# The low part of the keys in two score products: a contraction over 64 rows becomes one over 128

## The chip, the cores and the metric

The kernel runs on one core of a Trainium2 chip. The metric is the device time of one execution in microseconds (us). Lower is better. Engine names below are those of the profile: PE is TensorE's matmul, PEld its weight load, DVE is VectorE, ACT is ScalarE, POOL is GpSimd, SP is SyncE, which here only issues transfers.

## The reference

Two transformer blocks run one after the other on a sequence of 512 tokens of width 1024, all in float32. Two pieces of them matter here, the scores of the banded attention in the first block and those of the differential attention in the second:

```python
# first block: 8 query heads of width 64 on 2 key heads, a band of 128 tokens, a sink per head
s = jnp.einsum('bnqhgd,bnshd->bnhgqs', qb, kk) * (d ** -0.5)
s = jnp.where(mask[None, :, None, None], s, -jnp.inf)
p = jax.nn.softmax(jnp.concatenate([s, sink], axis=-1), axis=-1)[..., :-1]
...
# second block: 8 heads, each with two score maps (m) of width 64
s = jnp.einsum("bhmqd,bhmkd->bhmqk", qblk, kt) * scale
s = jnp.where(dist >= 0, s + bias[None, :, None], -jnp.inf)
p = jax.nn.softmax(s, axis=-1)
a = p[:, :, 0] - lam * p[:, :, 1]
return jnp.einsum("bhqk,bhkd->bhqd", a, vt)
```

Around them stand a forgetting attention in the first block, a causal convolution, a cross attention on 256 memory tokens and three gated projections in the second.

## The kernel before

All operands of the matmuls are split into a high and a low part of the type float32r, and a product is the sum of three: high by high, high by low, low by high. A score has a contraction of only 64, so its first matmul does two of the three at once. `q_stack` (L253 to L261) builds, for each half m of a 128-row tile, a tile whose 64 rows `a` hold the query's high part and whose other 64 rows `b` hold its low part. Beside it stands a key tile (`kb1`, `k1`) that holds the keys' high part in both halves. One matmul over 128 rows then gives high by high plus low by high. The third product, the query's high part by the keys' low part (`kbl`, `kl`), is a matmul of its own over the 64 rows `a` alone.

The banded attention (`swa_sc`, L640 to L667) goes over 2 key heads by 4 query blocks. A step has four pairs of such matmuls, L656 and L657, over 256 keys (128 in the first block). The differential attention (`diff_sc`, L1004 to L1023) goes over 8 heads by 4 query blocks n. A step has two pairs, L1012 and L1013, for m = 0 and m = 1, over (n + 1) * 128 keys. The forgetting attention (`fox_sc`, L736 and L737) has a pair of the same kind, only that its second matmul contracts over 68 rows. Each score lands in one of two PSUM banks (`sc_tile`), and VectorE empties it with one pass that adds the mask and takes the minimum (L658, L1015).

The instructions of each engine stand in a fixed order that a scheduler writes when the program is built. Code runs in `staged` steps (score, transposes one step later, the product with the values a step after that), and after each step `fill` advances generators that hold the large projections (`mm_T` L190, `mm_N` L199). So TensorE gets projection work between the pieces of an attention. VectorE's place in this order is shared by the softmax, the split of every weight into two parts (L171), and the convolution: 31 passes for each of 8 channel tiles (L893, L895), which the scheduler gives the lowest priority and spreads over the differential and the cross attention.

`diff_pro` (L982 to L1001) prepares a head: L992 makes the keys' low part `kl`, one VectorE pass over 128 rows. `xkv` (L1075 to L1087) loads the cross attention's keys and values of a head; the keys used the buffers of `kl` and the values a buffer of their own. `halves(m)` gives the rows `a` and `b`.

Of the kernel before, what the change touches and what calls it, by code (L numbers as in the profile page):

```python
# [11 lines left out]
F32 = mybir.dt.float32  # L12
# [3 lines left out]
ALU = mybir.AluOpType  # L16
# [43 lines left out]
class Fill:  # L60
# [6 lines left out]
    def first(self, name):  # L67
        i = [n for n, _ in self.q].index(name)
        if i > 1:
            x = self.q[i]  # L70
            del self.q[i]
            self.q.insert(1, x)
# [21 lines left out]
def two_block_kernel(ctx: ExitStack, tc: tile.TileContext, A: dict, out: bass.AP):  # L94
# [35 lines left out]
    def f(ap):  # L130
        return ap.bitcast(F32)
# [26 lines left out]

    # ---- weights: loaded in halves of the contraction, split into two float32r parts
    def load_w(src, w=CW, rp=None):  # L160
# [108 lines left out]
    def staged(items, first, second, last, lag, k):  # L269
        """first(item) at step i, second(item) at step i + lag, last(item) one step later."""  # L270
        n = len(items)
        for i in range(n + lag + 1):
            if i < n:
                first(items[i])
            if i - lag - 1 >= 0:
                last(items[i - lag - 1])
            if 0 <= i - lag < n:
                second(items[i - lag])
            fill(k(i) if callable(k) else k)
# [42 lines left out]

    # ---- norms, modulation, memory keys and values
    with ExitStack() as st:
# [95 lines left out]

        # rotary angles
        with low(-ROTP):
# [14 lines left out]

        # small per-kernel scalars
        first = dve.tensor_scalar(out=nsink, in0=V("sinks"), scalar1=-1.0, scalar2=None, op0=ALU.mult)
# [12 lines left out]

        # keys of the memory: normalised per head, transposed
        with low(LOWMK):
# [18 lines left out]

    # ---- first block
    stR = ExitStack()
# [59 lines left out]
    with ExitStack() as stS:  # L535
# [39 lines left out]

        # log of the sigmoid of the forget gate, summed along the tokens
        fs = fz.rearrange("p t h -> p (t h)")
# [62 lines left out]
        def swa_sc(it):  # L640
# [12 lines left out]
            for i in range(4):  # L653
                ps = sc_tile()
                r = slice(64 * (i % 2), 64 * (i % 2) + 64)
                pe.matmul(out=ps[:, :w], lhsT=qs[i][:, n * P:(n + 1) * P], rhs=kb1[g][:, j0 * P:j0 * P + w], start=True, stop=False)  # L656
                pe.matmul(out=ps[:, :w], lhsT=qs[i][r, n * P:(n + 1) * P], rhs=kbl[g][r, j0 * P:j0 * P + w], start=False, stop=True)  # L657
                dve.tensor_tensor_reduce(out=pt[:, i, :w], in0=ps[:, :w], in1=C("swam")[:, 256 - w:], scale=1.0,  # L658
                                         scalar=nsink[:, 4 * g + i:4 * g + i + 1], op0=ALU.add, op1=ALU.min, accum_out=mn[:, i:i + 1])
                act.activation(out=pt[:, i, :w], in_=pt[:, i, :w], func=AF.Exp, scale=-1.0, bias=mn[:, i:i + 1], accum_out=sm[:, i:i + 1])  # L660
# [129 lines left out]

    # the attention output in two float32r parts, on bytes that the attention no longer needs
    oh, ol = [None] * KT, [None] * KT
# [11 lines left out]

    # ---- output of the first block, two token tiles at a time
    with ExitStack() as st:
# [61 lines left out]

    # ---- second block: the three branches
    stV = ExitStack()  # L870
    cvp = open_pool(stV, "cvp", 2, side="right")
    with ExitStack() as st:
        wk = open_pool(st, "wk2", 2, reuse_waits="tile")
        dp = open_pool(st, "dp", 2, reuse_waits="tile")
        cm_[0] = open_pool(st, "cm2", 1, reuse_waits="tile")
        D = {}

        def glu_gen(m):
# [103 lines left out]
        def diff_pro(h):  # L982
# [5 lines left out]
            ps = transposed(kn, c0)  # L988
            kl = dp.tile([P, S], F32R, tag="kl", name="kl")
            ks = wk.tile([P, S], F32R, tag="ks", name="ks", bufs=1)  # L990
            act.activation(out=ks, in_=ps, func=AF.Copy, scale=gqk)
            dve.scalar_tensor_tensor(out=kl, in0=ps, scalar=gqk, in1=f(ks), op0=ALU.mult, op1=ALU.subtract)  # L992
            k1 = []
# [10 lines left out]
        def diff_sc(it):  # L1004
# [4 lines left out]
            for m in range(2):  # L1009
                a = halves(m)[0]  # L1010
                ps = sc_tile()
                pe.matmul(out=ps[:, :w], lhsT=q1[m][:, n * P:w], rhs=k1[m][:, :w], start=True, stop=False)  # L1012
                pe.matmul(out=ps[:, :w], lhsT=q1[m][a, n * P:w], rhs=kl[a, :w], start=False, stop=True)  # L1013
                p_ = wk.tile([P, S], F32, tag=f"dp{m}", name="dp", bufs=3 - m)
                dve.tensor_tensor_reduce(out=p_[:, :w], in0=ps[:, :w], in1=wb[:, S - w:], scale=1.0, scalar=FMAX,  # L1015
                                         op0=ALU.add, op1=ALU.min, accum_out=st_[:, 0, n, m:m + 1])
                act.activation(out=p_[:, :w], in_=p_[:, :w], func=AF.Exp, scale=-1.0, bias=st_[:, 0, n, m:m + 1], accum_out=st_[:, 1, n, m:m + 1])  # L1017
                pms.append(p_)
# [56 lines left out]
        def xkv(hd):  # L1075
            kr = dp.tile([P, 2, 256], F32, tag="kl", name="xkr")
            vr = dp.tile([P, 2, 256], F32, tag="xvr", name="xvr", bufs=1)
            nc.scalar.dma_start(out=kr, in_=kT_d[:, 2 * hd:2 * hd + 2, :])
# [132 lines left out]

    # ---- gates, projections, the weighted sum of the branches
    with ExitStack() as st:
# [219 lines left out]
```

## Time and profile before

| what | us |
|---|---|
| median of 3 runs | 1214.6 (1213.52 to 1215.86) |
| span of the profiled execution, first to last instruction | 1212.1 |
| TensorE busy | 1180.0 (97% of the span) |
| VectorE busy | 924.2 (76%) |
| ScalarE busy | 554.4 (46%) |
| GpSimd busy | 208.1 (17%) |

The profiled execution's own time is its span; the runs come out some 2.5 us above it, which is what lies before the first and after the last instruction, and what one execution differs from another. The banded attention lies at 131 to 204 us of the span, the forgetting attention at 217 to 313, the output of the first block up to 381, the differential attention's scores at 417 to 721, the cross attention up to 877, and after that come the projections of the three branches. TensorE's granted clock is at the higher of its two levels (2.4 GHz) from the banded attention to the end. A matmul's duration in the profile is longer than what it costs: matmuls follow each other before the one ahead has ended, so what a matmul costs is read from its start to the start of the next.

### The profile page before, as it was taken

The page shows a single profiled execution, that of the slowest core. Times are in us where ns is not written, and L with a number is a line of the kernel's source. Part 1 is how long each engine was busy: PE and PEld are TensorE (multiplying, and loading weights), DVE is VectorE, ACT ScalarE, POOL GpSimd, SP SyncE. Part 2 cuts the span into 40 slices and gives each one's busy share as a digit, 9 for nine tenths or more (in the row PEclk, how much of TensorE's full clock was granted, in tenths as well). Part 3 has the DMA queues.
Part 4 walks back from the last instruction along what each step waited for, and adds up shares of the span by engine and source line. Part 5 has one row for each costly group of instructions (what it writes and reads, how often), then busy time and mean ns, then how long its engine had stood idle before and what let it go on. Part 6 is the DMA issues. An engine that isn't in the chain of part 4 may idle for free.

```text
span 1212.1 us, 18966 instructions
## 1 busy us (share of the span) xinstructions
PE 1180.0 (97%) x6960; PEld 1018.9 (84%) x6960; DVE 924.2 (76%) x2047; ACT 554.4 (46%) x1173; POOL 208.1 (17%) x157
## 2 busy tenths in 40 slices
PE   7979999999999999999999999999999999999998
PEld 6868887878899988988888887988888888888898
DVE  6997766898776698998989989999793586553241
ACT  7556566557664354444545443543432245132230
POOL 1434200000021212020021221122010131111020
PEclk9989999999999999999999999999999999999999
DMA  8765312453474423323233333333446765432242
GB/s 334 263 214 153 98 49 74 150 158 109 128 238 150 125 70 97 104 88 113 88 112 90 111 107 122 112 106 122 148 134 215 268 207 190 124 104 89 88 125 83
DMA packets 61965, 165.43 MB, mean 136 GB/s; under 512 B 7120, under 2 KB 15568, under 8 KB 60848
## 3 DMA queue, kind: packets, MB, share of 16 engines
q1 hardware_dynamic: 36560, 122.41, 31.9%
q10 hardware_dynamic: 25312, 41.82, 10.0%
q8 instruction: 55, 0.90, 0.3%
q14 instruction: 38, 0.31, 0.1%
HBM read 136.80 MB, written 20.58 MB: 130 GB/s over the span
## 4 chain that ended last, share of the span: by engine, by line
PE 82%; DVE 7%; DMA 1%; issue 1%; ACT 1%; POOL 0%; ACTq 0%; POOLq 0%; DVEq 0%; SPq 0%
PE mm L190 46%; PE mm L199 22%; PE sc L1013 2%; PE tp L752 2%; DVE cv L895 1%; PE pv L1046 1%; PE sc L1012 1%; PE pv L695 1%; DVE wl L171 1%; PE tp L266 1%; PE pv L774 1%; PE sc L657 1%; PE pv L1191 1%; PE tp L240 1%; PE tp L225 1%
## 5 line engine op out<-in xcount | busy, mean ns | idle before, releaser
L169 ACT CAST wh<-raw 128x512 fp32r<-128x512 f32 x372 | 215.1, 620 | 226.5 <-PE mm L190 87.4
L171 POOL TENSOR_TENSOR wl<-raw,wh 128x512 fp32r<-128x512 f32 (+1 forms) x93 | 140.4, 1509 | 864.0 <-ACT wh L169 759.2
L171 DVE TENSOR_TENSOR wl<-raw,wh 128x512 fp32r<-128x512 f32 (+1 forms) x279 | 201.3, 747 | 99.7 <-ACT wh L169 99.0
L190 PE MATMUL mm<-hh,wh 128*128 128x512 f32 x640 | 255.9, 400 | 0.0
L190 PE MATMUL mm<-hl,wh 128*128 128x512 f32 x640 | 251.6, 393 | 0.0
L190 PE MATMUL mm<-hh,wl 128*128 128x512 f32 x640 | 251.6, 393 | 0.0
L895 DVE SCALAR_TENSOR_TENSOR cv<-u,vec,cv 128x512 f32<-128x512 f32 x240 | 192.4, 802 | 3.6
L199 PE MATMUL mm<-wh,hh 128*128 128x256 f32 (+1 forms) x672 | 193.4, 289 | 0.2 <-ACT hh L825 0.2
L199 PE MATMUL mm<-wl,hh 128*128 128x256 f32 (+1 forms) x672 | 190.7, 284 | 0.4 <-POOL wl L171 0.4
L199 PE MATMUL mm<-wh,hl 128*128 128x256 f32 (+1 forms) x672 | 190.8, 284 | 0.0
L190 PEld LDWEIGHTS mm<-hh,wl 128*128 128x128 f32 x640 | 120.3, 188 | 27.0
L190 PEld LDWEIGHTS mm<-hl,wh 128*128 128x128 f32 x640 | 120.6, 188 | 24.7
L190 PEld LDWEIGHTS mm<-hh,wh 128*128 128x128 f32 x640 | 120.5, 188 | 24.6
L199 PEld LDWEIGHTS mm<-wl,hh 128*128 128x128 f32 x672 | 128.4, 191 | 0.9 <-POOL wl L171 0.6
L199 PEld LDWEIGHTS mm<-wh,hh 128*128 128x128 f32 x672 | 128.0, 191 | 0.9 <-ACT hh L825 0.5
L199 PEld LDWEIGHTS mm<-wh,hl 128*128 128x128 f32 x672 | 128.2, 191 | 0.0
L190 PE MATMUL mm<-bh,wh 128*128 128x512 f32 x192 | 75.9, 396 | 0.0
L190 PE MATMUL mm<-bh,wl 128*128 128x512 f32 x192 | 75.4, 393 | 0.0
L190 PE MATMUL mm<-bl,wh 128*128 128x512 f32 x192 | 75.4, 393 | 0.0
L1017 ACT ACTIVATE dp<-dp,dst 128x128 f32<-128x128 f32 (+3 forms) x64 | 35.7, 559 | 42.1 <-DVE dst L1015 41.9
L199 PE MATMUL mm<-wl,mh 128*128 128x256 f32 x128 | 38.9, 304 | 7.4 <-DVE wl L171 7.4
L190 PEld LDWEIGHTS mm<-bl,wh 128*128 128x128 f32 x192 | 36.1, 188 | 8.4 <-issue 0.2
(327 smaller groups left out, 2121.7 us busy)
## 6 DMA issues: line engine op xcount, KB each, us to landing
raw<-in_w_dram SPq DMA_DIRECT2D x120, 512.0 KB
raw<-in_w_out_dram SPq DMA_DIRECT2D x24, 512.0 KB
raw<-in_w_mem_dram SPq DMA_DIRECT2D x16, 512.0 KB
ada<-in_w_ada_dram SPq DMA_DIRECT2D x8, 1024.0 KB
ada<-in_w_gate_dram SPq DMA_DIRECT2D x8, 512.0 KB
k<-ks SPq DMA_DIRECT2D x32, 128.0 KB
o_d<-sph ACTq DMA_DIRECT2D x16, 256.0 KB
o_d<-spl ACTq DMA_DIRECT2D x16, 256.0 KB
```

The source lines that it names most:

```text
L169: act.copy(out=wh[:, s], in_=raw[:, s])
L171: eng.tensor_tensor(out=wl[:, s], in0=raw[:, s], in1=f(wh[:, s]), op=ALU.subtract)
L190: m = pe.matmul(out=ps, lhsT=a[:, c0:c0 + P], rhs=at(b, k), start=(n == 0 and i == 0), stop=(n == KT - 1 and i == 2))
L199: pe.matmul(out=ps, lhsT=at(a, k)[:, t * P:(t + 1) * P], rhs=b[:, 0:n], start=(start and m == 0 and i == 0), stop=(stop and m == len(order ...
L225: m = pe.matmul(out=ps[:, t:t + 1], lhsT=sq[:, t * P:(t + 1) * P], rhs=ones[:, 0:1], start=True, stop=True)
L240: m = pe.matmul(out=ps[:, t * P:(t + 1) * P], lhsT=ones, rhs=dg[:, t, :], start=True, stop=True)
L266: pe.transpose(out=ps[:, t * P:(t + 1) * P], in_=src[:, t, c0:c0 + P], identity=ident)
L657: pe.matmul(out=ps[:, :w], lhsT=qs[i][r, n * P:(n + 1) * P], rhs=kbl[g][r, j0 * P:j0 * P + w], start=False, stop=True)
L752: pe.transpose(out=tp[:, j * P:(j + 1) * P], in_=pt_[:, j * P:(j + 1) * P], identity=ident)
L895: dve.scalar_tensor_tensor(out=a, in0=u[:, j:j + S], scalar=dw[:, m * 31 + j:m * 31 + j + 1], in1=a, op0=ALU.mult, op1=ALU.add)
L1013: pe.matmul(out=ps[:, :w], lhsT=q1[m][a, n * P:w], rhs=kl[a, :w], start=False, stop=True)
L1017: act.activation(out=p_[:, :w], in_=p_[:, :w], func=AF.Exp, scale=-1.0, bias=st_[:, 0, n, m:m + 1], accum_out=st_[:, 1, n, m:m + 1])
```

## The change

The second matmul of each pair contracts over all 128 rows. In the banded attention both halves of `kbl` already held the same keys, so only the slice goes. The query's low part then also meets the keys' low part. In the differential attention the low part of each half m gets a tile of its own, `klz`, with zeros in the other 64 rows. Four such tiles (two heads by two halves) are allocated once and their zero halves are written by GpSimd at the start of the second block; a head then writes its low part in two passes over 64 rows instead of one over 128. The cross attention's keys and values, which needed the old buffers, now use the same four tiles. Lines that only lose a comment are left out.

```diff
@@ swa_sc
             for i in range(4):
                 ps = sc_tile()
-                r = slice(64 * (i % 2), 64 * (i % 2) + 64)
                 pe.matmul(out=ps[:, :w], lhsT=qs[i][:, n * P:(n + 1) * P], rhs=kb1[g][:, j0 * P:j0 * P + w], start=True, stop=False)
-                pe.matmul(out=ps[:, :w], lhsT=qs[i][r, n * P:(n + 1) * P], rhs=kbl[g][r, j0 * P:j0 * P + w], start=False, stop=True)
+                pe.matmul(out=ps[:, :w], lhsT=qs[i][:, n * P:(n + 1) * P], rhs=kbl[g][:, j0 * P:j0 * P + w], start=False, stop=True)
@@ second block
         D = {}
+        klz = []
+        for i in range(2):
+            pair = []
+            for m in range(2):
+                z = dp.tile([P, S], F32R, name=f"klz{i}{m}", bufs=1)
+                pool.memset(f(z[halves(m)[1]]), 0.0)
+                pair.append(z)
+            klz.append(pair)
@@ diff_pro
-            kl = dp.tile([P, S], F32R, tag="kl", name="kl")
             ks = wk.tile([P, S], F32R, tag="ks", name="ks", bufs=1)
             act.activation(out=ks, in_=ps, func=AF.Copy, scale=gqk)
-            dve.scalar_tensor_tensor(out=kl, in0=ps, scalar=gqk, in1=f(ks), op0=ALU.mult, op1=ALU.subtract)
+            kl = klz[h % 2]
+            for m in range(2):
+                a = halves(m)[0]
+                dve.scalar_tensor_tensor(out=kl[m][a], in0=ps[a], scalar=gqk[a], in1=f(ks[a]), op0=ALU.mult, op1=ALU.subtract)
@@ diff_sc
             for m in range(2):
-                a = halves(m)[0]
                 ps = sc_tile()
                 pe.matmul(out=ps[:, :w], lhsT=q1[m][:, n * P:w], rhs=k1[m][:, :w], start=True, stop=False)
-                pe.matmul(out=ps[:, :w], lhsT=q1[m][a, n * P:w], rhs=kl[a, :w], start=False, stop=True)
+                pe.matmul(out=ps[:, :w], lhsT=q1[m][:, n * P:w], rhs=kl[m][:, :w], start=False, stop=True)
@@ xkv
-            kr = dp.tile([P, 2, 256], F32, tag="kl", name="xkr")
-            vr = dp.tile([P, 2, 256], F32, tag="xvr", name="xvr", bufs=1)
+            kr, vr = (f(z).rearrange("p (k c) -> p k c", k=2) for z in klz[hd % 2])
             nc.scalar.dma_start(out=kr, in_=kT_d[:, 2 * hd:2 * hd + 2, :])
             nc.scalar.dma_start(out=vr, in_=v_d[:, :, hd * 256:(hd + 1) * 256])
```

TensorE's order, at the third query block of a head in the differential attention, before. `sc` is a score bank, `kl` the low part, `qs` the query's tile.

```order
L199 MATMUL mm<-wh,hl 128x256
L1012 MATMUL sc<-k_5070,qs 128x384
L1013 MATMUL sc<-kl,qs 128x384
L1012 MATMUL sc<-k_5073,qs 128x384
L1013 MATMUL sc<-kl,qs 128x384
L225 MATMUL tp<-cst,doq 128x1 x4
L752 MATMUL tp<-cst,dp 128x128 x2
```

The same place in the changed kernel:

```order
L199 MATMUL mm<-wh,hl 128x256
L1022 MATMUL sc<-k_5078,qs 128x384
L1023 MATMUL sc<-klz_4541,qs 128x384
L1022 MATMUL sc<-k_5081,qs 128x384
L1023 MATMUL sc<-klz_4543,qs 128x384
L225 MATMUL tp<-cst,doq 128x1 x4
L751 MATMUL tp<-cst,dp 128x128 x2
```

Nothing moved: through the whole program TensorE has the same instructions in the same order, and only the tile that the second matmul reads is another.

VectorE's order where a head is prepared, before. `qs` is a half of the query's stack, `cv` a pass of the convolution, and the ISA rows empty the score banks.

```order
L893 TENSOR_SCALAR cv<-u,vec 128x512
L259 SCALAR_TENSOR_TENSOR qs<-tp,qs 64x512
L992 SCALAR_TENSOR_TENSOR kl<-tp,gqk,ks 128x512
L259 SCALAR_TENSOR_TENSOR qs<-tp,qs 64x512
L895 SCALAR_TENSOR_TENSOR cv<-u,vec,cv 128x512
L1015 ISA dp,dst<-sc,wb 128x128
L1015 ISA dst 128x1
L895 SCALAR_TENSOR_TENSOR cv<-u,vec,cv 128x512
L1015 ISA dp,dst<-sc,wb 128x128
```

And in the changed kernel:

```order
L902 TENSOR_SCALAR cv<-u,vec 128x512
L259 SCALAR_TENSOR_TENSOR qs<-tp,qs 64x512
L1003 SCALAR_TENSOR_TENSOR klz_4541<-tp,gqk,ks 64x512
L259 SCALAR_TENSOR_TENSOR qs<-tp,qs 64x512
L1003 SCALAR_TENSOR_TENSOR klz_4543<-tp,gqk,ks 64x512
L1025 ISA dp,dst<-sc,wb 128x128
L1025 ISA dst 128x1
L1025 ISA dp,dst<-sc,wb 128x128
L1025 ISA dst 128x1
```

One pass over 128 rows became two over 64, and here two passes of the convolution went to a later place. Over the eight heads VectorE has eight instructions more. The number of convolution passes ahead of the end of each head's scores differs by two at most, and is the same (124) at the end of the last head.

ScalarE's order where the last head's scores end and the cross attention's second head is loaded, before. `xkr` and `xvr` are its keys and values, `xh` their high part.

```order
L169 CAST wh<-raw 128x512 x4
L1084 CAST xh<-xkr 128x512
L754 CAST pth<-tp 128x3x128
L1017 ACTIVATE dp,dst<-dp,dst 128x512 x2
L1084 CAST xh<-xvr 128x512
L1078 DMA xkr<-kT_d 128x512
```

And in the changed kernel:

```order
L169 CAST wh<-raw 128x512 x4
L1087 DMA klz_4541<-kT_d 128x512
L1027 ACTIVATE dp,dst<-dp,dst 128x512 x2
L753 CAST pth<-tp 128x3x128
L1088 DMA klz_4543<-v_d 128x2x256
L1093 CAST xh<-klz_4541 128x512
L1087 DMA klz_4541<-kT_d 128x512
L1093 CAST xh<-klz_4543 128x512
```

The loads of the second head's keys and values, which stood some thirty instructions earlier, now stand behind the last scores, and the casts right behind the loads.

## Rows read from the trace of the kernel before

**Rows 1.** The page's part 4: the chain that ended last, by engine.

```profile
PE 82%; DVE 7%; DMA 1%; issue 1%; ACT 1%; POOL 0%; ACTq 0%; POOLq 0%; DVEq 0%; SPq 0%
```

**Rows 2.** Who waited, TensorE, 400 to 730 us: total, times, longest.

```profile
PE tp L752 <- DVE dp L1022: 0.5, 1, 0.5
```

**Rows 3.** Windows: stretch, length, busy time (instructions) of PE, PEld, DVE, ACT, POOL.

```profile
120.00:210.00 90.00, 90.00 (x502) 72.47 (x501) 64.39 (x189) 53.68 (x140) 12.10 (x14) 1.00 0.25 76
...
420.00:460.00 40.00, 40.00 (x254) 34.55 (x254) 39.19 (x88) 18.95 (x44) 8.86 (x5) 1.00 0.24 66
460.00:500.00 40.00, 40.00 (x261) 35.10 (x261) 34.86 (x88) 19.02 (x44) 2.66 (x2) 1.00 0.39 120
...
620.00:660.00 40.00, 40.00 (x268) 35.34 (x266) 33.31 (x84) 19.59 (x44) 3.96 (x2) 1.00 0.39 113
660.00:700.00 40.00, 40.00 (x209) 32.70 (x209) 39.27 (x97) 18.31 (x42) 9.29 (x6) 1.00 0.36 112
```

**Rows 4.** Timeline of PE, a score step over 512 keys: start, duration, instruction.

```profile
719.64 0.40 PE L1012 MATMUL sc<-k,qs 128*128 128x512 f32 x1
719.96 0.50 PE L1013 MATMUL sc<-kl,qs 64*128 64x512 f32 x1
720.39 0.50 PE L1012 MATMUL sc<-k,qs 128*128 128x512 f32 x1
720.83 0.50 PE L1013 MATMUL sc<-kl,qs 64*128 64x512 f32 x1
721.26 0.33 PE L752 MATMUL tp<-cst,dp 128*128 128x128 f32 x1
```

**Rows 5.** Timeline of the weight loads at the same place.

```profile
719.41 0.19 PEld L1012 LDWEIGHTS sc<-k,qs 128*128 128x128 f32 x1
719.96 0.18 PEld L1013 LDWEIGHTS sc<-kl,qs 64*128 64x128 f32 x1 [0.36 <-issue]
```

**Rows 6.** Timeline of PE, a score step over 128 keys, its first and the next instruction.

```profile
491.04 0.22 PE L1012 MATMUL sc<-k,qs 128*128 128x128 f32 x1
...
491.96 0.38 PE L240 MATMUL tp<-rdiag,cst 128*128 128x128 f32 x1
```

**Rows 7.** Timeline of PE, pairs of the forgetting attention: 128, 256 and 512 keys.

```profile
216.89 0.23 PE L736 MATMUL sc<-k,qs 128*128 128x128 f32 x1
...
217.06 0.45 PE L190 MATMUL mm<-hh,wh 128*128 128x512 f32 x1
...
219.89 0.28 PE L736 MATMUL sc<-k,qs 128*128 128x256 f32 x1
...
220.13 0.41 PE L190 MATMUL mm<-hh,wh 128*128 128x512 f32 x1
...
226.16 0.39 PE L736 MATMUL sc<-k,qs 128*128 128x512 f32 x1
226.39 0.40 PE L737 MATMUL sc<-k,q 68*128 68x512 f32 x1
226.64 0.38 PE L752 MATMUL tp<-cst,fp 128*128 128x128 f32 x2
```

**Rows 8.** Timeline of PE, two pairs of the banded attention, and the next instruction.

```profile
157.35 0.28 PE L656 MATMUL sc<-kb,qs 128*128 128x256 f32 x1
...
158.50 0.45 PE L695 MATMUL pv<-sph,vbh 128*64 128x512 f32 x1
```

**Rows 9.** Lines L259 and L992: count, ns min/median/max, first and last start, forms.

```profile
L259 DVE SCALAR_TENSOR_TENSOR qs<-tp,qs x24: 674/685/694, 129.0 to 651.0; 64x512 fp32r<-64x512 f32 x24
...
L992 DVE SCALAR_TENSOR_TENSOR kl<-tp,gqk,ks x8: 750/750/751, 409.3 to 650.3; 128x512 fp32r<-128x512 f32 x8
```

**Rows 10.** Timeline of POOL, its first instruction in the second block.

```profile
387.60 1.30 POOL L171 TENSOR_TENSOR wl<-raw,wh 128x512 fp32r<-128x512 f32 x1 [20.05 <-ACT wh L169]
```

**Rows 11.** Timeline of ACT: the load of a head's keys, and their cast.

```profile
680.66 0.33 ACTq L1078 DMA_DIRECT2D xkr<-kT_d  x1
...
685.93 0.62 ACT L1084 CAST xh<-xkr 128x512 fp32r<-128x512 f32 x1 [1.23 <-DMA xkr<-kT_d]
```

## The prediction

> **What bounds the kernel now.** I read the chain of waits first: 82% of it is TensorE, 7% VectorE [rows 1]. Then who waited for whom: over the whole differential attention TensorE waited 0.5 us, once, for a softmax pass of VectorE [rows 2]. So TensorE's own stream of instructions sets the time in the stages that the change touches, and what a matmul there costs comes off the end, as long as no other engine takes over. Which engine that could be, the windows show. In the banded attention VectorE is busy 64.4 of 90 us, with room to spare. In the differential attention it is a different picture: windows of 40 us alternate between nearly full (39.19 and 39.27 of 40) and lighter ones (34.86 and 33.31) [rows 3]. Four windows are of the heavy kind and four of the light between 420 and 740 us. TensorE is at 40.00 in nearly all of them. VectorE is thus a second bound just behind the first.
>
> Last the timeline, from start to start. A score step over 512 keys has four matmuls, and takes 719.64 to 721.26, 1.62 us, 0.32 to 0.44 each [rows 4]. The forgetting attention's pair over as many keys, whose second matmul contracts over 68 rows, takes 226.16 to 226.64, 0.48 us, so 0.24 each [rows 7]. The columns are the same, the operand types are the same, and the profile shows no wait in either. What differs is that L1013 is shown as 64*128 and L737 as 68*128 in a stream that is otherwise 128 rows. The weight load tells how: L1012's load begins at 719.41, 0.23 ahead of its matmul, under the matmul before, while L1013's load begins only at 719.96, together with its own matmul, after 0.36 us in which no load ran and none was held by a semaphore [rows 5]. The load and the way in and out of the 64-row form are paid in the open, on both sides of every such matmul.
>
> **The change part by part.** *TensorE, differential attention.* The order of instructions is the same, so each step's four matmuls stay together. A step costs 0.92 us over 128 keys [rows 6] and 1.62 over 512 [rows 4], and the two widths between lie evenly, so 1.27 on average. Two forgetting pairs cost 2 x 0.17 over 128 and 2 x 0.48 over 512 [rows 7], 0.65 on average. With 128 rows everywhere I take that price: 0.62 less per step, by 32 steps 19.8 us, 2.5 us for each of the 8 heads. The bounds of this term: nothing, if the number of rows is not what costs; and 19.8, since nothing in the stream is cheaper than the full-row rate.
>
> *TensorE, banded attention.* Two pairs over 256 keys take 157.35 to 158.50, 0.575 each [rows 8]; a forgetting pair over 256 takes 0.24 [rows 7]. Pairs that stand alone between other matmuls will save a little less than the 0.335, as a neighbour outside then shares the way in; I take 0.30 for the 24 of them, and for the 8 over 128 keys 0.46 - 0.17 = 0.29 (half a differential step, [rows 6]). That is 9.5 us. VectorE empties the two score banks; with the pairs arriving faster, the third pair of a step may find its bank still full. VectorE has a quarter of its time free there [rows 3], so I take off 0.5 and keep 9.0. Its bounds are 0 and 9.5, like above.
>
> *VectorE.* Two passes over 64 rows replace one over 128. A pass of this kind over 64 rows takes 0.685 us and one over 128 takes 0.750 [rows 9]: the rows don't shorten it. So 2 x 0.685 - 0.750 = 0.62 us more per head, 5.0 in all, on the engine that is the second bound. A heavy window holds about one head: VectorE's work becomes 39.2 + 0.6 = 39.8 us where TensorE would now need 40 - 2.5 = 37.5. A light one becomes 35.5 against 37.5. So in the light windows TensorE still leads and the saving is kept, and in the heavy ones VectorE falls 2.3 us behind. What is late next then is the softmax's output: the transposes (L752) wait for it, and with them everything queued on TensorE. Part of the lateness can be carried into the following light window, where VectorE gains 2.0. How much is not shown by any row directly; that TensorE already had to wait once for a softmax pass [rows 2] says that in the tightest place there is nothing to carry. Between 0 and 2.0 I take 0.8, and for VectorE's own short waits, of which 0.8 us were left in a heavy window, half. That makes a loss of 2.3 - 0.8 + 0.4 = 1.9 in each of four heavy windows, 7.5 us. Bounds: 0, when all is carried, and 4 x (2.3 + 0.8) = 12.4, when nothing is and the waits stay.
>
> *Edits I cost at nothing.* The four zero fills go to GpSimd, which stands idle for 20.05 us ahead of 387.60 [rows 10]; at no more than the 1.30 of a two-operand pass each they take up to 5.2 us, under that gap. Were the cover gone, 5.2 us would fall on that split of a weight. The cross attention's loads come later: the values of its first head now wait for the seventh head's tile, and both loads of the second head for the last scores. A load took from 680.66 to 685.93, 5.3 us, until its cast could run, of which ScalarE waited 1.23 [rows 11]. At the second head the load and cast stand closer together, so I allow ScalarE up to 5 us of waiting there, behind which the copy of the last transposes is queued. ScalarE is busy only 19 of 40 us [rows 3]; I take 0 and keep up to 3 us for the range.
>
> **Sum.** 9.0 + 19.8 - 7.5 = 21.3 us. The profiled span 1212.1 becomes 1190.8, and the median 1214.6, which lies 2.5 above the span, 1193.3.
>
> **A rule that speaks against it.** The Trainium skill, "TensorE: Matmul & The Clock Gate", says in the section "Why this matters for your kernels" that a lone matmul over few rows takes as long as one over 128, and that the profit of few rows is that matmuls in different row groups run side by side. By that the change saves nothing, and gives up a chance, since the two halves m lie in different row groups. The trace doesn't agree: 0.43 against 0.24 us, and the two 64-row matmuls of a step start 0.87 apart [rows 4], with a 128-row one between them, so nothing runs side by side that could be lost.
>
> **The rivals.** *All of it arrives:* VectorE's lateness is carried over, because its order can slip by a few us against TensorE's without a stall. For it: 0.5 us of waiting in the whole stage. Against: the heavy windows have 0.8 us free for 2.9 us of missing room. The time would be 1214.6 - 28.8 = 1186.
>
> *VectorE takes most of it:* nothing is carried, the waits stay, and shorter stretches inside the light windows are full too. The heavy windows then give nothing (0.6 longer each than before), the light ones half of their 2.5: 9.0 + 5 - 2.4 = 11.6, so 1203.
>
> *Slower:* the open load and the gaps have another cause than the 64 rows, such as the low part's tile or the accumulation into the bank of the matmul before. TensorE then saves nothing, while VectorE's 0.62 per head falls on heavy windows that have 0.8 free: up to 5.0 us, 1217 to 1219. It decides from the point where a 128-row L1013 still takes over 0.40 us from start to start. Against it: the forgetting pair accumulates in the same way at 0.24.
>
> *No change:* the same, with VectorE's extra hidden, or the rule above: 1214.6.
>
> **How the numbers follow.** Forecast 0.60 (its own range 1188.5 to 1198.5, from the bounds of VectorE's loss, 2.5 to 12.4, and 0.5 for the rest), all of it 0.16, VectorE takes most 0.18, slower 0.03, no change 0.03. The range takes in the two neighbours: 1184 to 1203. A difference of 0.2%, 2.4 us, is about what a measurement of this kernel can tell from none. Faster 0.94, same 0.03, slower 0.03.
>
> **What will show it.** Right, if the changed line stands as 128*128 and a step over 512 keys takes about 0.95 us; if its weight load begins with the matmul ahead of it; if the two low-part passes take 0.69 each; if VectorE is above 99% in the heavy windows and TensorE waits there for VectorE, some 5 to 10 us in total, at L751. Wrong, if TensorE shows no such waits (then nearer 1186), if the steps stay above 1.4 us, or if ScalarE's casts hold up the cross attention.

## The result, and the profile after

The changed kernel takes **1195.0 us** (median of 4, 1193.7 to 1196.6) against 1214.1 for the kernel before (median of 4): a ratio of 0.9833, 95% interval [0.982, 0.9846], 19.1 us less. Forecast was 1193.3. The profiled execution is the longest of the four: it took 1196.6, with a span of 1194.8 where before had 1212.1, so 17.3 less. Line numbers are those of the changed kernel: L1012 and L1013 have become L1022 and L1023, L656 to L658 are L655 to L657, L992 is L1003, L752 is L751, L755 is L754, L1022 is L1032, L895 is L904, L1129 is L1138.

The steps first. The timeline of PE at a score step over 512 keys, the counterpart of [rows 4]:

```profile
700.71 0.39 PE L1022 MATMUL sc<-k,qs 128*128 128x512 f32 x1
700.94 0.40 PE L1023 MATMUL sc<-klz,qs 128*128 128x512 f32 x1
701.17 0.39 PE L1022 MATMUL sc<-k,qs 128*128 128x512 f32 x1
701.40 0.39 PE L1023 MATMUL sc<-klz,qs 128*128 128x512 f32 x1
701.63 0.49 PE L751 MATMUL tp<-cst,dp 128*128 128x128 f32 x3
```

and the weight loads at the same place, the counterpart of [rows 5]:

```profile
700.49 0.19 PEld L1022 LDWEIGHTS sc<-k,qs 128*128 128x128 f32 x1
700.71 0.19 PEld L1023 LDWEIGHTS sc<-klz,qs 128*128 128x128 f32 x1
```

A step is 0.92 us in place of 1.62. The load of the low part begins at 700.71, with the matmul ahead of it, 0.23 before its own; before, it began with its own matmul after 0.36 us without a load. Over the four widths the median steps, those with a wait behind them left out, are 0.40, 0.47, 0.70 and 0.93 us, which is 0.62 on average against 1.26: 0.64 less, 20.5 us in 32 steps (forecast 19.8).

Not all of that arrives. The chain of waits by engine, the counterpart of [rows 1]:

```profile
PE 63%; DVE 24%; issue 3%; ACT 1%; DMA 0%; POOL 0%; ACTq 0%; DVEq 0%; POOLq 0%
```

Who waited, TensorE from 380 to 745 us, where [rows 2] had one wait of 0.5:

```profile
PE tp L266 <- DVE ptl L754: 2.9, 2, 1.6
PE tp L240 <- DVE xql L1138: 2.5, 1, 2.5
PE tp L240 <- DVE qs L259: 2.0, 3, 1.0
PE tp L751 <- DVE rt L213: 1.2, 1, 1.2
PE tp L751 <- DVE dp L1032: 1.0, 2, 0.7
PE pv L1056 <- DVE ptl L754: 0.4, 1, 0.4
PE tp L225 <- DVE qs L259: 0.4, 1, 0.4
```

and the windows (PE, PEld, DVE, ACT, POOL busy, granted clock), as in [rows 3]:

```profile
410.00:450.00 40.00, 39.71 (x280) 36.95 (x279) 39.66 (x93) 18.62 (x44) 6.12 (x4) 1.00 0.29 80
450.00:490.00 40.00, 37.06 (x256) 33.93 (x255) 37.59 (x90) 19.59 (x46) 5.18 (x4) 1.00 0.40 124
490.00:530.00 40.00, 39.91 (x284) 37.41 (x283) 39.85 (x92) 18.17 (x40) 9.15 (x5) 1.00 0.21 69
530.00:570.00 40.00, 37.63 (x259) 34.13 (x258) 38.28 (x94) 19.48 (x47) 2.62 (x2) 1.00 0.44 125
```

The heavy windows (410 to 450 and 490 to 530 among those shown) are at 99 to 100% of VectorE, and all of TensorE's waits are for it: 7.9 us from 380 to 730, where the forecast took 7.5. They do not lie where the forecast put them, though. In the four heavy windows from 410 to 730 TensorE waits 1.5 us in all, in the four lighter ones 6.4: TensorE is busy 39.71 and 39.91 of 40 in the two heavy windows shown and only 37.06 and 37.63 in the lighter ones behind them. VectorE's lateness is carried over the end of the heavy window and paid there. And only 1.0 is the softmax's output at the transposes; the rest is mostly at those who need a transpose bank, and once behind a step of a norm's inverse root (L213). One place shows how. VectorE, in its order, as a head begins:

```profile
480.73 0.69 DVE L259 SCALAR_TENSOR_TENSOR qs<-tp,qs 64x512 fp32r<-64x512 f32 x1
481.45 0.74 DVE L1003 SCALAR_TENSOR_TENSOR klz<-tp,gqk,ks 64x512 fp32r<-64x512 f32 x1
482.22 0.69 DVE L259 SCALAR_TENSOR_TENSOR qs<-tp,qs 64x512 fp32r<-64x512 f32 x1
482.95 0.76 DVE L1003 SCALAR_TENSOR_TENSOR klz<-tp,gqk,ks 64x512 fp32r<-64x512 f32 x1
```

and TensorE there:

```profile
483.06 1.13 PE L240 MATMUL tp<-rdiag,cst 128*128 128x128 f32 x8 [0.99 <-DVE qs L259]
```

L240 needs a transpose bank, and TensorE waits 0.99 for the second split of the queries, which ends at 482.91. That split stands behind the first of the two new passes (0.74), as it stood behind the single pass of 0.75 before, so this alone is not new; what the second pass changes shows in the one-tile run below.

The last loss is behind the stage, where the sum had nothing. TensorE at the first queries of the cross attention:

```profile
733.93 0.40 PE L190 MATMUL mm<-hh,wh 128*128 128x512 f32 x1
736.84 1.32 PE L240 MATMUL tp<-rdiag,cst 128*128 128x128 f32 x8 [2.51 <-DVE xql L1138]
...
740.10 0.63 PE L190 MATMUL mm<-hl,wh 128*128 128x512 f32 x1
740.53 0.63 PE L190 MATMUL mm<-hh,wl 128*128 128x512 f32 x1
```

VectorE there:

```profile
733.88 2.31 DVE L904 SCALAR_TENSOR_TENSOR cv<-u,vec,cv 128x512 f32<-128x512 f32 x3
736.10 1.28 DVE L1138 SCALAR_TENSOR_TENSOR xql<-tp,xqh 128x512 fp32r<-128x512 f32 x2
```

and the windows at that place:

```profile
733.00:737.00 4.00, 1.47 (x7) 0.88 (x7) 3.93 (x8) 0.56 (x2) 0.00 (x0) 1.00 0.45 139
737.00:739.00 2.00, 2.00 (x13) 2.00 (x14) 1.84 (x4) 0.00 (x0) 0.00 (x0) 0.67 0.08 29
739.00:741.00 2.00, 2.00 (x10) 1.81 (x9) 1.88 (x4) 0.62 (x1) 0.00 (x0) 0.50 0.00 0
```

Three passes of the convolution stand ahead of the queries' split, TensorE waits 2.51 us (1.0 in the trace of before), and behind that wait its granted clock is 0.67 on average and then 0.50 of full speed, the lower of its two levels: an L190 then goes 0.43 from start to start in place of 0.23. That costs 2 x 0.33 + 2 x 0.50 = 1.7 us more. The same place in the runs below: a wait of 2.6 us and a clock of 0.83 from 740 to 750 in the run of the differential edit alone; waits of 1.0 and 0.4 and no fall in the one-tile run and the one with half the convolution. But a fall does not follow from the wait's length alone: in the run that moves two convolutions out of the differential attention, TensorE waits as long at this place,

```profile
PE tp L240 <- DVE xql L1138: 2.5, 1, 2.5
```

and its clock stays at 1.00 from 731 to 740.

The account, stage by stage, as the lead of TensorE's stream over that of before: banded attention 7.8 (forecast 9.0), output stage of the first block -1.0, differential attention 12.9 (forecast 19.8 - 7.5 = 12.3), cross attention -2.5 net (1.5 of longer waiting and some 1.7 of lower clock, less 0.7 for a wait on GpSimd that only the kernel before has). That is 17.2 of the 17.3 by which the spans differ. The -1.0 is no effect of the change as far as the runs show: from the first matmul of the first block's output to the first score of the second block the profiled execution takes 117.3 us and before 116.3, but the two runs of the changed kernel with another order of the fill work, whose code is the same up to there, take 116.1 and 116.3.

### The profile page after: what moved, and what is told of

It is laid out like the page before. It is cut to its first block, busy times and chain, and to the rows that moved or that the text cites. A ratio compares the mean times of both kernels' runs of the same rounds, so it can differ in the third digit from the quotient of the medians.

```text
span 1194.8 us, 18995 instructions
## 1 busy us (share of the span) xinstructions
PE 1154.0 (97%) x6960; PEld 1015.9 (85%) x6960; DVE 926.6 (78%) x2055; ACT 551.7 (46%) x1173; POOL 213.3 (18%) x161
## 4 chain that ended last, share of the span: by engine, by line
PE 63%; DVE 24%; issue 3%; ACT 1%; DMA 0%; POOL 0%; ACTq 0%; DVEq 0%; POOLq 0%
PE mm L190 40%; PE mm L199 15%; DVE cv L904 7%; DVE wl L171 3%; DVE dp L1025 1%; PE pv L773 1%; DVE dp L1032 1%; PE tp L751 1%; DVE dp L1031 1%; DVE ptl L754 1%; PE sc L1157 1%; PE pv L694 1%; PE pv L1200 1%; DVE qs L259 1%; PE tp L266 1%
## 5 line engine op out<-in xcount | busy, mean ns | idle before, releaser
L190 PE MATMUL mm<-hh,wh 128*128 128x512 f32 x640 | 255.9, 400 | 0.0
L190 PE MATMUL mm<-hh,wl 128*128 128x512 f32 x640 | 251.8, 393 | 0.0
L190 PE MATMUL mm<-hl,wh 128*128 128x512 f32 x640 | 251.7, 393 | 0.0
L904 DVE SCALAR_TENSOR_TENSOR cv<-u,vec,cv 128x512 f32<-128x512 f32 x240 | 191.1, 796 | 3.4
L190 PEld LDWEIGHTS mm<-hh,wl 128*128 128x128 f32 x640 | 120.5, 188 | 27.0
L190 PEld LDWEIGHTS mm<-hh,wh 128*128 128x128 f32 x640 | 120.6, 188 | 24.7
L190 PEld LDWEIGHTS mm<-hl,wh 128*128 128x128 f32 x640 | 120.8, 189 | 24.5
L190 PE MATMUL mm<-bh,wh 128*128 128x512 f32 x192 | 75.9, 396 | 0.0
L190 PE MATMUL mm<-bh,wl 128*128 128x512 f32 x192 | 75.4, 393 | 0.0
L190 PE MATMUL mm<-bl,wh 128*128 128x512 f32 x192 | 75.4, 393 | 0.0
L190 PEld LDWEIGHTS mm<-bl,wh 128*128 128x128 f32 x192 | 36.1, 188 | 8.4 <-issue 0.2
```

The source lines that it names most:

```text
L190: m = pe.matmul(out=ps, lhsT=a[:, c0:c0 + P], rhs=at(b, k), start=(n == 0 and i == 0), stop=(n == KT - 1 and i == 2))
L904: dve.scalar_tensor_tensor(out=a, in0=u[:, j:j + S], scalar=dw[:, m * 31 + j:m * 31 + j + 1], in1=a, op0=ALU.mult, op1=ALU.add)
```

## The experiments

The theory: a matmul over 64 rows costs its way in and out of that form, the change takes this away, and VectorE's load takes part back. The main rivals: the two edits share a bound; the order of VectorE's passes, not their amount, makes TensorE wait. Times are medians; the kernel before ran beside each group at 1214.2, 1214.8 and 1214.7.

### The two edits apart

The first run is the kernel before with

```
-                r = slice(64 * (i % 2), 64 * (i % 2) + 64)
...
-                pe.matmul(out=ps[:, :w], lhsT=qs[i][r, ...], rhs=kbl[g][r, ...], start=False, stop=True)
+                pe.matmul(out=ps[:, :w], lhsT=qs[i][:, ...], rhs=kbl[g][:, ...], start=False, stop=True)
```

> The kernel before with the edit of the banded scores alone (L657 over all 128 rows); the differential scores stay at 64 rows. Theory: the low-part matmul over 64 rows is what costs, and a pair of 256 keys falls from 0.575 to about 0.24-0.30 us; the trace of the changed kernel has its TensorE stream 7.8 us ahead at the end of this stage, of which the output stage of the first block gives back up to 1.0. So 1206 to 1207.5, and no more than 1 us lost after that. Rival, that the stage is held by its softmax and the lead is given back in the second block: 1211 or more. Rival, that each edit alone gives nothing without the other: 1214.

1206.8 us, ratio 0.9935 [0.9921, 0.9948]: 7.4 less, as expected. The second run is the changed kernel without this edit.

> The changed kernel with the banded scores put back to 64 rows, so that only the differential edit is left, with its second VectorE pass, its zero fills and its shared buffers. Theory: TensorE's stream gains 12 to 13 us over the differential attention (19.8 of matmul time less 6 to 8 of waits for VectorE), and gives back 2 to 3 at the cross attention's queries, so 1203.5 to 1205. Together with the run of the banded edit alone the two gains should add up to the 19.0 of the whole change within 1 us. Rival, that the two edits share a bound, so that together they are worth less than apart: 1201 or less here.

1203.4 us, ratio 0.9911 [0.9897, 0.9924]: 10.8 less, at the lower edge of what was expected. Together 18.2 against 19.1: they add up, within what these medians can tell. Their shares are not those of the matmul time saved (20.5 to 8.4), since VectorE takes back mostly in the differential stage.

### One tile of low keys in place of two

The changed kernel's TensorE stream without its extra VectorE passes:

```
-                pe.matmul(out=ps[:, :w], lhsT=q1[m][a, n * P:w], rhs=kl[a, :w], start=False, stop=True)
+                pe.matmul(out=ps[:, :w], lhsT=q1[m][:, n * P:w], rhs=kl[:, :w], start=False, stop=True)
```

> The kernel before with the banded edit, and the differential low-part matmul over all 128 rows of the one old tile of low keys: beside the wanted half's rows stand the other half's low keys in place of zeros. That adds, to each score, the product of the query's low part with the other half's low keys, which the product otherwise leaves out. No second VectorE pass, no zero fills, and the cross attention's buffers as in the kernel before. TensorE's instructions are those of the changed kernel. Theory: what the changed kernel does not get of the 19.8 is VectorE's time, and 0.62 us less of it per head shortens the waits: 1190 to 1192.5, with TensorE's waits for VectorE over the differential attention down from 7.9 to 3 to 5 us. Rival, that the waits come from the order in which VectorE's passes stand and not from its load: 1194 to 1196, the waits as in the changed kernel.

1194.8 us, ratio 0.9837 [0.9824, 0.985]: the changed kernel's time to 0.3 us, so the theory lost this one. Who waited, TensorE from 380 to 745 us, the largest of 9.5 us and one of the small ones:

```profile
PE tp L751 <- DVE rt L213: 2.3, 1, 2.3
PE pv L1044 <- DVE ptl L754: 2.1, 2, 1.1
PE tp L751 <- DVE dp L1020: 1.7, 2, 1.4
PE tp L240 <- DVE xql L1127: 1.0, 1, 1.0
...
PE tp L240 <- DVE kl L991: 0.2, 1, 0.2
```

The waits for the queries' split (L259) are gone, as the missing pass should bring. The last line shows how: at the place where the changed kernel waits 0.99 for the second split, TensorE here waits 0.19, and for the single low-part pass (L991, to 481.16), which stands ahead of that split. With the low part in two passes the second ends only at 483.71, behind the split, so by the releasers that the profile names the first bank to come free is now the split's, 0.7 us later in VectorE's order. But other waits have grown: the sum is 9.5 in place of 10.4. The windows show VectorE as full as ever (39.77 of 40 from 410 to 450, 39.86 from 490 to 530), since the convolution, 30 passes of 0.75 us for each channel tile, has moved up. VectorE's instructions at the first score step, in their order, in the changed kernel (-) and here (+):

```
-L1025 ISA dp,dst<-sc,wb 128x128
-L1025 ISA dst 128x1
-L1025 ISA dp,dst<-sc,wb 128x128
-L1025 ISA dst 128x1
-L904 SCALAR_TENSOR_TENSOR cv<-u,vec,cv 128x512
+L894 SCALAR_TENSOR_TENSOR cv<-u,vec,cv 128x512
+L1013 ISA dp,dst<-sc,wb 128x128
+L1013 ISA dst 128x1
+L894 SCALAR_TENSOR_TENSOR cv<-u,vec,cv 128x512
+L1013 ISA dp,dst<-sc,wb 128x128
+L1013 ISA dst 128x1
```

A convolution pass now stands ahead of each of the two score passes. Taking away the prediction's "0.62 us more per head, 5.0 in all" thus brings nothing: the zeros, the second pass and the shared buffers together cost nothing that can be measured in this order of the work. (This rests on the medians. The two profiled spans differ by 2.1 us, about what the changed kernel's trace loses to the fall of the clock, which this run does not have.)

### The two 64-row matmuls side by side

The kernel before, all shapes as they were, with the step's matmuls in another order:

```
+            pss_ = [sc_tile() for m in range(2)]
+            for m in range(2):
+                pe.matmul(out=pss_[m][:, :w], lhsT=q1[m][:, n * P:w], rhs=k1[m][:, :w], start=True, stop=False)
             for m in range(2):
                 a = halves(m)[0]
-                ps = sc_tile()
-                pe.matmul(out=ps[:, :w], lhsT=q1[m][:, n * P:w], rhs=k1[m][:, :w], start=True, stop=False)
-                pe.matmul(out=ps[:, :w], lhsT=q1[m][a, n * P:w], rhs=kl[a, :w], start=False, stop=True)
+                pe.matmul(out=pss_[m][:, :w], lhsT=q1[m][a, n * P:w], rhs=kl[a, :w], start=False, stop=True)
```

> The kernel before, all matmuls in their old shapes, with the four matmuls of a differential score step in another order: first the two over 128 rows, then the two over 64, one right behind the other. Theory, that the price is paid on the way into the 64-row form and out of it, once each per stretch: one way in and out fewer per step, about 0.29 us, by 32 steps 9 us on TensorE, of which VectorE takes 0 to 2 back, as its load does not change: 1205 to 1208, with a step over 512 keys at 1.30 to 1.36 us in place of 1.62. Rival, that each 64-row matmul costs by itself, wherever it stands: no change, 1214. Rival, that the two in different row groups run side by side: the second starts within 0.1 us of the first, a step over 512 keys at 1.15 or less, and 1202 or less.

1204.1 us, ratio 0.9911 [0.9898, 0.9925]. The timeline of PE at a step over 512 keys:

```profile
710.51 0.63 PE L1011 MATMUL sc<-k,qs 128*128 128x512 f32 x2
711.07 0.51 PE L1014 MATMUL sc<-kl,qs 64*128 64x512 f32 x2
711.50 0.55 PE L752 MATMUL tp<-cst,dp 128*128 128x128 f32 x3
```

and its weight loads:

```profile
711.07 0.18 PEld L1014 LDWEIGHTS sc<-kl,qs 64*128 64x128 f32 x2 [0.36 <-issue]
711.50 0.20 PEld L752 LDWEIGHTS tp<-cst,dp 128*128 128x128 f32 x2 [0.25 <-issue]
```

Two matmuls from 711.07 on are done within 0.51 us, where one alone took 0.50 [rows 4]; in all 32 steps the second starts 3 to 4 ns after the first, and both loads start there too. They run side by side: the third expectation. From 710.51 to 711.50 the four take 0.99, of which three full matmul times are 0.69 and some 0.30 is the way in and out, once. Over the widths the median steps are 0.52, 0.64, 0.81 and 0.99, 0.74 on average, 0.52 less than before or 16.7 us in 32 steps, most of what the change saves, without a zero. Of this 10.0 arrive, which is 2 us short of the expected "1202 or less": TensorE waits 5.0 us for VectorE from 380 to 745, where it waited 0.5 before. In the trace 10.5 us arrive over this stage; the 1.6 that neither this nor the waits account for are mostly delays of 0.1 to 0.3 us each, at places such as L1046 and L266, too short for the list of waits.

So the rule of the Trainium skill that the prediction weighed ("TensorE: Matmul & The Clock Gate", "Why this matters for your kernels": matmuls over few rows in different row groups run side by side) holds in this trace for neighbours. Its other half, that a lone one takes as long as one over 128 rows, does not hold for one of 64 rows between 128-row ones: 0.43 to 0.24.

### VectorE relieved by leaving out half of the convolution

```
-                for j in range(1, 31):
+                for j in range(1, 16):
```

in the kernel before and in the changed one.

> The kernel before with the convolution cut from 31 taps to 16, so that half of the convolution is left out and VectorE has some 80 us less to do in the second block; all matmuls as before. It is the partner of the next run. Theory: TensorE sets the time of the kernel before in these stages, so VectorE's relief is worth only the waits that it had there (0.5 and 1.0 us): 1212 to 1214.5. Rival, that VectorE held the kernel before too: 1209 or less.

> The changed kernel with the convolution cut from 31 taps to 16 in the same way (half of the convolution left out). Theory, that what the change did not bring was taken back by VectorE's load: its distance to the partner run, the kernel before cut alike, grows from 19 to 26 to 29 us, so 1184.5 to 1187, without waits of TensorE for VectorE over the differential attention and without a fall of the clock at the cross attention's queries. Rival, that the waits come from the order of VectorE's passes in a chain that no relief shortens: the distance stays at 18 to 21, so 1192 to 1195.

Before so cut: 1213.5 us, 0.9984 [0.9975, 0.9993]. Changed and so cut: 1187.8, 0.9776 [0.9763, 0.979]. The distance has grown from 19.1 to 25.7, a little under the 26 to 29 expected. So VectorE's load, above all the convolution's, took back 6.6 us of the change, and the kernel before, to which the same relief is worth 1.4, paid next to nothing for it. In the traces the lead that TensorE gains over the differential attention is 17.8 us in place of 12.9, and the cross attention, which took 2.5 back, now takes nothing. Who waited in the changed one, TensorE in the whole execution, the lines of this stage:

```profile
PE tp L751 <- DVE dp L1032: 2.0, 3, 1.0
PE tp L240 <- DVE qs L259: 2.0, 3, 1.0
...
PE tp L240 <- DVE xql L1138: 0.4, 1, 0.4
PE pv L1056 <- DVE ptl L754: 0.4, 1, 0.4
```

5.0 us in place of 10.4, counted from 380 to 860 in both, and no fall of the clock at the queries. What is left are the queries' split, as long as in the changed kernel (2.0), and the softmax's output. "Without waits" was wrong. Whether the one-tile form, which has no waits at the split, would gain them here was not tested.

### GpSimd takes more of the weight splits

```
-                eng = pool if q and j else dve
+                eng = pool if j and (q or wide) else dve
```

with `wide` set in the second block's branches alone, in the changed kernel and in the one-tile form.

> The changed kernel with GpSimd taking half of all splits of the second block's weights in place of a quarter, so one pass fewer on VectorE per weight; nothing is left out. Theory, that VectorE's load is what holds TensorE: the 10 us of waits between 380 and 745 us fall below 5, and 1187 to 1191. Rival, that the order holds it, or that GpSimd's slower pass makes a weight late: 1194 or more.

> The run with one tile of low keys for both halves (the other half's low keys in place of zeros, a term that the product otherwise leaves out, in the scores), and GpSimd taking half of the second block's weight splits as in the run beside it. In the first form alone, taking the two extra VectorE passes per head away was worth nothing measurable (1194.77 against 1195.02). Theory, that load counts only where it stands ahead of a late pass: with the splits moved, 1187 to 1190, within 2 us of the run beside it. Rival, that both reliefs add up once VectorE is no longer full: 1185 or less.

1214.3 us (0.9995 [0.9987, 1.0004]) and 1214.8 (0.9998 [0.9989, 1.0007]): the whole gain of the change is lost in both, far beyond the first rival's "1194 or more", and against all that was expected of the second. In the first run TensorE waits 22.2 us from 380 to 860, in place of 10.4. VectorE has 39 instructions fewer (2016 to 2055), which at 0.69 each should save 27 us, and is busy 928.8 us in place of 926.6. Its timeline tells why:

```profile
668.77 1.24 DVE L1033 TENSOR_TENSOR drr<-drr,nlam 128x1 f32<-128x1 f32 x1
...
676.88 1.17 DVE L1033 TENSOR_TENSOR drr<-drr,nlam 128x1 f32<-128x1 f32 x1
...
688.66 0.15 DVE L1033 TENSOR_TENSOR drr<-drr,nlam 128x1 f32<-128x1 f32 x1
```

with GpSimd's beside it:

```profile
666.43 3.57 POOL L173 TENSOR_TENSOR wl<-raw,wh 128x512 fp32r<-128x512 f32 x2
676.74 1.29 POOL L1097 TENSOR_TENSOR xl<-klz,xh 128x512 fp32r<-128x512 f32 x1 [6.74 <-ACT xh L1096]
```

L1033 works on one column and takes 0.15 at 688.66. At 676.88, begun 0.14 into a pass of GpSimd (one that the changed kernel has there too), it takes 1.17 and ends with that pass; at 668.77, under weight splits of GpSimd (L173), it takes 1.24 and ends with them as well. The convolution's pass takes 0.75 alone and 1.23 on average where a GpSimd pass of two operands ran beside it (46 of 240; 28 in the changed kernel). So a split moved from VectorE (0.69) to GpSimd (1.5) holds VectorE for about as long as it frees it, and it does so at the short passes of the softmax. The Trainium skill says this ("SBUF — State Buffer", "SBUF: two separate sides": the port pair that the two engines share is locked for a whole instruction); the trace agrees. That this alone makes up the 19 us was not separated: the moved passes also change VectorE's order, and the clock is below full speed in three of the 40 us windows.

### The fill work in another order

The fourth tile of the convolution changes places with matmuls that bring VectorE little:

```
-... dqk3 dg2 dv3 glu3 xq0 dg3 xg0 xq1 glu4 m11 glu5 m12 glu6 m13 glu7 m20 m21 m22 m23
+... dqk3 dg2 dv3 m11 xq0 dg3 xg0 xq1 glu3 glu4 m12 glu5 m13 glu6 m20 glu7 m21 m22 m23
```

in the changed kernel, in the one-tile form, and in the kernel before as the control; a further order takes two tiles out.

> The changed kernel with the list of the second block's fill work in another order and nothing left out: the fourth channel tile of the gated convolution (glu3) changes places with a gate's matmuls (m11) that are as long on TensorE and bring VectorE no convolution, and the other convolutions come later by as much. In the changed kernel the 30 passes of a convolution fill each of the four heavy windows. Theory, that these passes stand ahead of the softmax's and the queries' work on VectorE: the waits from 620 to 745 us (0.5, 1.2, 0.7 and 2.5, and 1.6 at a halved clock behind the last) fall to 2 or less, so 1190 to 1192.5. Rival, that the waits are VectorE's own chains, with or without a convolution: within 1.5 of 1195. Rival, that the later convolutions crowd the cross attention: 1197 or more.

> The kernel before with that same order of fill work (one convolution moved), as the control. Theory: TensorE sets the kernel before there, with 0.5 us of waits to win and 1.0 at the cross attention's queries, so 1212.5 to 1215, and the change is worth more under this order than its 19. Rival, that the order is better or worse by itself whatever the scores cost: the same step as between the changed kernel and its reordered form.

1203.0 us (0.9903 [0.989, 0.9917]), 7.9 worse than the changed kernel; the control 1222.9 (1.0071 [1.0058, 1.0085]), 8.2 worse than before. The order costs both 0.7%, as the rivals had it, so the change itself is worth the same under it. The trace of the first shows that the theory's own part was right, in two windows without a convolution and one behind them:

```profile
610.00:650.00 40.00, 40.00 (x270) 36.70 (x269) 31.69 (x85) 22.47 (x49) 4.73 (x3) 1.00 0.44 134
650.00:690.00 40.00, 40.00 (x246) 35.95 (x245) 26.08 (x75) 19.93 (x44) 7.82 (x6) 1.00 0.38 117
...
770.00:810.00 40.00, 34.67 (x204) 30.08 (x203) 37.83 (x68) 16.12 (x33) 8.07 (x5) 0.91 0.31 107
```

TensorE is full and VectorE has 8 and 14 us to spare from 610 to 690, where the changed kernel waits 1.7. But the convolutions then stand in the cross attention. TensorE there:

```profile
803.29 0.79 PE L1200 MATMUL pv<-xpth,xh 128*128 128x512 f32 x1 [4.10 <-ACT xo L1203]
```

The copy L1203, which frees the bank, is queued on ScalarE behind

```profile
801.74 0.47 ACT L1163 ACTIVATE xp<-sc,xst 128x256 f32<-128x256 f32 x1 [4.56 <-DVE xst L1161]
```

and the L1161 that this waits for starts on VectorE at 801.03, behind three passes of the convolution and three weight splits since 796.00. At this wait, too, the clock falls (0.91 in the window): it is at 0.96 from 800 to 802, still within the wait, and at 0.50 from there to 808. Between 740 and 900 us TensorE waits 5.8, where the changed kernel shows none from 745 to 860.

> The same with two convolutions taken out of the differential attention (the second of the heavy windows and the last), two gates' matmuls in their places. Theory: half of the waits go there, 1188 to 1191. Rival, that VectorE then has no room for six convolutions behind it, and the layer norm that needs all eight comes late: 1196 or more, with TensorE waiting behind 900 us, where the changed kernel shows no wait.

1232.5 us (1.0145 [1.0131, 1.0158]): the last convolution ends at 984, and the layer norm that needs all eight leaves TensorE waiting 34.3 us behind 1000, at the lower clock in part:

```profile
1020.00:1040.00 20.00, 4.05 (x17) 3.60 (x17) 16.50 (x37) 9.98 (x17) 0.00 (x0) 0.50 0.00 0
```

> The one-tile form (the other half's low keys in place of zeros, an added term in the scores) with the order of the run with one convolution moved. Theory, that the second low-part pass holds the queries' split back by its 0.7 us wherever VectorE isn't otherwise full (the waits at L259 of 2.0 and 0.4 in the changed kernel, none in the one-tile form): once the convolution is out of the way, it is worth 1 to 2.5 us against the zeros with the same order. Rival: no difference, within 0.7 us.

1200.5 us (0.9884 [0.9867, 0.9901]), 2.5 less than with the zeros in the same order, as the theory had it; but the intervals of the two overlap, so this is a hint. No version that leaves nothing out beat the changed kernel by more than its scatter.

## Why the prediction was right, point by point

**The 64-row form is what costs.** Right, and shown from three sides: the changed step is at the full-row rate, the two edits apart each bring their part, and with all shapes kept a step loses most of the price when its two 64-row matmuls stand together (16.7 of 20.5). The term for the differential steps was 19.8 and measures 20.5.

**The banded attention** was put at 9.0 and measures 7.8. The direction of the deduction was right, the score banks come free late at L655; its size was about 1.7 in place of 0.5 (the pairs save 8.4 us from start to start in place of 9.5). Of the 1.7, 0.8 is shown as waits of the matmul (both at L655, for L657); L655's weight load waits 3.6 us more for the same pass, in nine places, part of it under the matmul ahead.

**VectorE takes 7.5 back.** That VectorE takes over where TensorE is faster was right, and the size came out (7.9 of waits from 380 to 730). The working did not, so the size is in part luck. It had 1.9 lost in each heavy window and the saving kept in the light ones; measured are 1.5 in the four heavy windows together and 6.4 in the four light ones, so the lateness is carried over the window's end, and not made good there. It had the change's own 0.62 us per head fall on the heavy windows; taking these passes away brings nothing measurable, as the convolution moves up into what is free. Halving the convolution brings 6.6, part of it in the cross attention, so it is mainly its passes, in the way of short ones that TensorE needs sooner than before, that make VectorE late. And the waits are not at L751 alone, as the prediction said, but mostly at the users of a transpose bank.

**Edits at nothing.** The zero fills take 0.52 us each, 2.1 in all, under GpSimd's idle time, less than the 5.2 allowed; with the one-tile run, which has neither fills nor shared buffers, at the same time, nothing of this part shows.

**Left out of the sum:** the cross attention gives 2.5 back in the profiled execution, by one longer wait and the fall of the clock behind it, and the output stage of the first block 1.0, which looks like scatter. With 1.2 less from the banded attention and 0.6 more from the differential one this explains why that execution gained 17.3 and not the forecast 21.3; the median gained 19.1. Whether the other executions had the same fall of the clock has no trace: their mean granted clocks are 0.993, 0.994 and 0.996, against 0.991, and do not go with their times (1193.7, 1194.8 and 1195.2).

**The rivals.** All of it arriving (1186) is what the kernel comes near with half of the convolution left out (1187.8). A slower kernel would have needed an L1023 over 0.40 us from start to start; it is 0.23.

## What to carry to other kernels

A matmul over 64 rows alone between full ones pays 0.26 to 0.34 us for its form here (half of what a step saves, over 128 to 512 keys): fill it to 128 rows with zeros (or with rows that do no harm), or put two in different halves of the rows next to each other, which costs some 0.1 us more per step of four here than the zeros. When the bound is taken down by a few per cent, ask which long rows of filler work on the second engine stand ahead of short passes that are waited for; moving them elsewhere, or to GpSimd, has to be paid where they arrive. And look at the clock behind a wait: in one trace a wait of 2.5 us cost 1.7 more, in another an equal one cost nothing more.

## What the runs showed of the hardware that was not expected

Two 64-row matmuls in different halves start together (3 to 4 ns apart) and finish in the time of one. GpSimd's two-operand pass of 1.29 us stretches a VectorE pass of 0.15 us to 1.17, up to its own end. And TensorE's clock went to the lower level at single waits of 2.51 us (just behind it) and 4.10 us (within it), and stayed there for 3 to 5 us of full work, while another wait of 2.51 us, in the run that moves two convolutions, left it at 1.00.
